# A two-layer hybrid trunk: the FFN's third sums behind the operand's low halves, and the last tile's order of products and stores

## The chip, the cores and the metric

One core of a Trainium2 chip runs the whole program. The metric is the time of one execution on the device, in microseconds (us); lower is better. The core has a matrix engine (TensorE, PE in the profile), a vector engine (VectorE, DVE), an activation engine (ScalarE, ACT), GpSimd (POOL) and SyncE (SP), which issues most transfers. Each engine works through its own queue in order, and they meet through semaphores. SBUF is the memory on the chip, PSUM holds the sums of TensorE.

## What is computed

512 tokens of width 1024 pass through two layers. Cut to what the change touches:

```
x = x + merged @ w_o[i]
h = rmsnorm(x, norm_ffn[i])
x = x + (silu(h @ w_ffn_gate[i]) * (h @ w_ffn_up[i])) @ w_ffn_down[i]
h = rmsnorm(x, norm_ple[i])
x = x + sigmoid(h @ w_ple_gate[i]) * (p[i] @ w_ple_in[i])
...
return rmsnorm(x, norm_final)
```

`merged` comes from an attention, a convolution and a neighbourhood attention under gates; the FFN is 2816 wide. All data are float32.

## The kernel before, in words

**Precision.** An fp32 operand is split into a high half, rounded by ScalarE, and a low half, the rest, made by VectorE (`split`, `operand`). A product is then three matmuls: high by high, high by low, low by high (`mm3`, lines 177 to 179; `product` in `seven`, 983 to 985; `products` in `final`, 1204 to 1206). Activations lie with features on the 128 partitions and 512 tokens along the row, in eight blocks.

**w_o.** `w_o` multiplies the merged operand with eight blocks of output features. The first two blocks go as a pair: 42 matmuls for the first seven operands of both, then the eighth operand, whose halves are the last to be made (the tile mergeb_v, written from gatec_x). Each finished block is added to x, split for the FFN, and squared for the norm. After blocks 2, 4 and 6 `quarters` forms four sums of the operand's blocks (its t1 to t4) and splits them; the last of the four calls stands at the beginning of the FFN.

**FFN.** The 22 blocks of 128 features go in three parts (8, 7, 7). The first block of a part is a plain pair, the gate and the up product. For the others, `seven` gets both products over halves of the tokens and of the inner width from seven half-size products instead of eight, with sums of weights: `s1` and `s2` (up's lower half added to pieces of gate and up by an accumulating transfer of the POOL queue, line 955), and the third sums `s3` = `s1` + a22 (a22 being up's upper half, tile ffn_r) and `s4` = `s3` + the gate's upper half (tile ffn_wr). `s3` and `s4` lie in one place (half of an ffn_qk tile), shared by all blocks, and are split into the tiles ffn_pt or ffn_y.

**What sets the order.** PE's queue is the order of the code. The other engines' queues are set by a planner that knows estimated costs and priorities: weight work is raised in priority (`high_priority`) so that it is placed ahead of the stage that needs it. `behind(i, then)` adds an edge that orders two instructions of one engine without a semaphore. In `seven` the edge puts `s3` behind a22's split, and, where `first` is set (the first such block of parts two and three), behind `self.held`, the last low half of the block before.

**The last tile.** The last layer's final 256 features are computed with tokens on the partitions, in four tiles of 128 tokens (`final`). For a tile: eight times three gate products (`products`), six input products (`inputs`, into PSUM's sc), four transposes of finished features (`chunks`, into tr), and the transposes of 512 more (`low`). `finish` takes the sigmoid on ScalarE, multiplies, adds and sums the squares on VectorE and takes the power -0.5 on GpSimd (line 1228): the column. `store` scales the row by it, on ScalarE for 512 features (line 1235), on VectorE for 256 and 256 (line 1237, which the profile shows under its helper's line 160, and line 1238), and stores each half with one transfer, from the ACT queue (line 1236) and from SP (line 1239).

Of the kernel before, what the change touches and what calls it, by code (L numbers as in the profile page):

```python
# [15 lines left out]
ALU = mybir.AluOpType  # L16
# [9 lines left out]
D = 1024  # L26
# [35 lines left out]
class Net:  # L62
# [848 lines left out]
    def quarters(self, x, h, j):  # L911


        one, two = slice(0, 256), slice(256, 512)
        g = lambda k: self.par(self.i, "ffn", k)
        f = []
        for k in (2 * j, 2 * j + 1):
            v = self.sb("t", [P, 512])
            self.act(v, x[k], AF.Copy, scale=g(k))
            f.append(v)  # L920
        b11, b12, b21, b22 = f[0][:, one], f[0][:, two], f[1][:, one], f[1][:, two]
        u = self.sb("t", [P, 2, 256])
        w = self.sb("t", [P, 2, 256])
        t1, t2, t3, t4 = u[:, 0], u[:, 1], w[:, 0], w[:, 1]
        self.tt(t1, b11, b12, ALU.subtract)
        self.tt(t2, b22, t1, ALU.add)
        self.tt(t3, b22, b12, ALU.subtract)
        self.tt(t4, t2, b21, ALU.subtract)
        if j < 2:
            d = [self.sb("rp" if n < 2 else "e", [P, 2, 256], F32R) for n in range(4)]  # L930
        else:
            d = [q for n in range(2) for q in self.zs[2 * j - 4 + n]]
        for o, t in zip(d, (t1, t2, t3, t4)):
            self.split(o[:, 0], o[:, 1], t)
        ha, hb = self.halves(h[2 * j]), self.halves(h[2 * j + 1])
        cut = lambda p, c: (p[0][:, c], p[1][:, c])
        return dict(b11=cut(ha, one), b21=cut(hb, one), b22=cut(hb, two),
                    **{f"t{n + 1}": (o[:, 0], o[:, 1]) for n, o in enumerate(d)})

    def seven(self, wg, wu, bs, tags, spare, md, first):  # L940


        nc = self.nc
        with self.tc.high_priority(offset=min(self.w_ahead, self.tc.cur_priority - self.p0)):
            lo, up = slice(0, 512), slice(512, 1024)
            g, a22 = self.sb("wr", [P, 1024]), self.sb("r", [P, 512])
            sums = self.sums[self.sevens % 3], self.sums[3]
            self.sevens += 1
            s1, s2, s3, s4 = (s[:, q:q + 512] for s in sums for q in (0, 512))
            nc.sync.dma_start(s1, wg[:, lo])  # L950
            nc.sync.dma_start(s2, wu[:, up])
            nc.sync.dma_start(g, wg)
            nc.sync.dma_start(a22, wu[:, up])
            for q in (s1, s2):
                nc.gpsimd.dma_start(q, wu[:, lo], accum_op=ALU.add)  # L955
            ws = {}

            def halve(hi, lo, src, names):
                i = self.split(hi, lo, src)
                for q, name in enumerate(names):  # L960
                    c = slice(q * 512, q * 512 + 512)
                    ws[name] = (hi[:, c], lo[:, c])
                return i

            wide = lambda: (self.sb("wh", [P, 1024], F32R), self.sb("wl", [P, 1024], F32R))
            halve(*wide(), g, ("a11", "a12"))
            low = halve(self.sb("kh", [P, 512], F32R), self.sb("a", [P, 512], F32R), a22, ("a22",))
            halve(*wide(), sums[0], ("s1", "s2"))
            i = self.tt(s3, s1, a22, ALU.add)
            self.behind(i, low)  # L970
            if first:
                self.behind(i, self.held)
            self.tt(s4, s3, g[:, up], ALU.add)
            halve(*spare, sums[1], ("s3", "s4"))
# [64 lines left out]
    def ffn(self, h, x):  # L1039
        self.phase = "ffn"  # L1040
        i = self.i
# [5 lines left out]
        for part in PARTS:  # L1047
            mids = []
            for f, fb in enumerate(part):
                tags = (("mm", "mm", "mm"), ("sc", "sc", "av"))[fb % 2]  # L1050
                md = md8[f]
                mids.append(md)
                wg, wu = self.a["w_fg"][i, fb], self.a["w_fu"][i, fb]
                if fb:
                    self.seven(wg, wu, bs, tags, spare[fb % 2], md, part[0] and f < 2)
                    continue
                g = self.sb("t", [P, 512])
                pg, pu = (self.ps(t) for t in tags[:2])
                for j in range(len(QUARTERS), 4):
                    self.four.append(self.quarters(x, h, j))  # L1060
                self.pair((pg, pu), (wg, wu), [h[k] for k in ORDER])

                def gate(pg=pg, g=g):
                    self.tt(g, pg, self.rb, ALU.mult)
                    self.act(g, g, AF.Silu, table="silu")

                self.ready(gate)

                def up(pu=pu, g=g, md=md):
                    self.tt(g, g, pu, ALU.mult)  # L1070
                    self.split(md[:, 0, :], md[:, 1, :], g)

                self.ready(up)
# [103 lines left out]
    def final(self, h, x, pairs, hn, most):  # L1177
# [36 lines left out]
        def finish(t):  # L1214
            g = self.sb("t", [P, 256])
            self.act(g, pgs[t], AF.Sigmoid, table="sigmoid", scale=rbs[:, t:t + 1])
            self.tt(g, g, pis[t], ALU.mult)
            v = self.sb("a", [P, 256])
            self.tt(v, g, pair[t][:, 256:], ALU.add)
            q = self.sb("t", [P, 256])  # L1220
            s = self.sb("s", [P, 1])
            nc.vector.tensor_tensor_reduce(
                out=q, in0=v, in1=v, scale=1.0, scalar=0.0, op0=ALU.mult, op1=ALU.add,
                accum_out=s)
            ms = self.sb("sm", [P, 1])
            self.stt(ms, s, 1.0 / D, part[:, t:t + 1], ALU.mult, ALU.add)
            col = self.sb("rc", [P, 1])
            nc.gpsimd.tensor_tensor(col, ms, self.power[:, 0:1], ALU.pow)
            vs.append(v)
            columns.append(col)  # L1230

        def store(t):
            col, two = columns[t], pair[t]
            r, out = rows[t], self.a["out"][t * P:(t + 1) * P]
            self.act(r[:, 0:512], low[t], AF.Copy, scale=col)
            nc.scalar.dma_start(out[:, 0:512], r[:, 0:512])
            self.stt(r[:, 768:], vs[t], col, self.gain, ALU.mult, ALU.mult)
            nc.vector.tensor_scalar(r[:, 512:768], two[:, 0:256], col, None, ALU.mult)
            nc.sync.dma_start(out[:, 512:], r[:, 512:])

        pair, low, pgs, vs, columns = [], [], [], [], []
        places = ("av", "mm", "av", "sc")
        def inputs(t):
            pis.append(self.ps("sc", (P, 256)))
# [6 lines left out]
        for t in range(4):  # L1251
# [10 lines left out]
            if t == 1:  # L1262
# [3 lines left out]
                       start=True, stop=True)  # L1266
                part = self.sb("sm", [P, 4])
                nc.vector.tensor_scalar(part, sums, 1.0 / D, EPS, ALU.mult, ALU.add)
            if t:
                chunks(t)  # L1270
            if t > 1:
                inputs(t)
            products(pg, wg, h, t, range(6, 8))
            pgs.append(pg)
            if t == 1:
                finish(0)
# [130 lines left out]
```

## Time and profile before

| | us |
|---|---|
| time, median of 3 runs (lowest to highest) | 1793.07 (1792.29 to 1793.09) |
| profiled execution, its own time | 1792.81 |
| its span, from first to last instruction | 1791.0 |
| PE busy | 1774.5 |
| DVE busy | 1410.6 |
| ACT busy | 891.6 |
| POOL busy | 99.3 |
| DMA, mean | 142 GB/s |

A row of a time line gives the start (us from the span's start), the duration, the engine, the line of the kernel, the operation, the tile written and the tiles read with shapes, and in brackets the idle time of the engine before it with what ended it. Tiles carry the name of their stage: wo_mm is a PSUM tile of the w_o stage, ffn_qk an SBUF tile of the FFN. Matmuls overlap: one of 512 columns is shown with 0.39 us, and the next starts 0.23 us behind it. "SPq" and "ACTq" are transfers issued by these queues. Line numbers are those of the kernel before.

### The profile page before, as it was taken

What the parts mean: (1) busy time and instruction counts of PE and PEld (TensorE: products, weight loads), DVE (VectorE), ACT (ScalarE), POOL (GpSimd) and SP (SyncE); (2) the same over time, 40 slices, a digit from 0 to 9 for tenths busy, and PEclk for the clock granted to TensorE, in tenths of its full rate; (3) what the DMA queues carried; (4) which work ended last, traced back from release to release, by engine and by line L of the source; (5) the groups of instructions that cost most, each with busy time, mean ns of one, the idle gap of its engine ahead of it and who ended that gap; (6) DMA issues with size and microseconds to landing.
All of it is one profiled execution on the core that took longest, in us unless ns stands there. A gap on an engine that the chain in (4) does not pass through costs nothing.

```text
span 1791.0 us, 27255 instructions
## 1 busy us (share of the span) xinstructions
PE 1774.5 (99%) x10138; PEld 1559.7 (87%) x10138; DVE 1410.6 (79%) x2394; ACT 891.6 (50%) x1551; POOL 99.3 (6%) x142
## 2 busy tenths in 40 slices
PE   9999999999999999999999999999999999999998
PEld 7888888888799899998888888888887998989987
DVE  7877888997788587787776788889887885877776
ACT  5577555325565254454535765552355652534444
POOL 0000000000111011100000000000001110101000
PEclk9999999999999999999999999999999999999999
DMA  5665541334747365544447655422356563746332
GB/s 206 190 182 169 159 124 46 108 98 150 217 130 188 111 166 154 140 123 127 145 125 200 170 161 148 112 71 95 97 182 186 153 173 108 182 133 159 98 103 94
DMA packets 112212, 254.48 MB, mean 142 GB/s; under 512 B 14416, under 2 KB 19024, under 8 KB 112080
## 3 DMA queue, kind: packets, MB, share of 16 engines
q1 hardware_dynamic: 99264, 229.40, 41.9%
q0 software_dynamic: 12096, 22.03, 7.8%
q8 instruction: 80, 1.31, 0.3%
q10 hardware_dynamic: 720, 1.31, 0.2%
q14 instruction: 52, 0.43, 0.1%
HBM read 213.89 MB, written 7.34 MB: 124 GB/s over the span
## 4 chain that ended last, share of the span: by engine, by line
PE 91%; DVE 4%; DMA 2%; ACT 2%; issue 1%; SPq 0%; DVEq 0%; POOLq 0%; ACTq 0%
PE ffn_mm L177 5%; PE ffn_mm L178 5%; PE ffn_mm L179 5%; PE ffn_mm L985 4%; PE ffn_mm L984 4%; PE ffn_mm L983 4%; PE ffn_sc L985 3%; PE ffn_sc L984 3%; PE ffn_sc L983 3%; PE mergea_mm L178 2%; PE mergea_mm L179 2%; PE mergea_mm L177 2%; PE diff_sc L784 2%; PE gatec_mm L177 2%; PE gatec_mm L178 2%; PE gatec_mm L179 2%
## 5 line engine op out<-in xcount | busy, mean ns | idle before, releaser
L160 DVE SCALAR_TENSOR_TENSOR conv_z<-glu_z,pre_par,conv_z 128x512 f32<-128x512 f32 x240 | 179.6, 748 | 3.3
L143 ACT ACTIVATE ffn_wh<-ffn_wr 128x1024 fp32r<-128x1024 f32 (+1 forms) x94 | 94.9, 1015 | 110.0 <-PE ffn_mm L178 75.1
L157 DVE TENSOR_TENSOR ffn_wl<-ffn_wr,ffn_wh 128x1024 fp32r<-128x1024 f32 (+1 forms) x94 | 109.9, 1174 | 5.1 <-ACT ffn_wh L143 4.6
L955 POOL DMA_DIRECT2D ffn_qk<-w_fu x84 | 74.6, 996 | 550.5 <-DMA ffn_qk<-w_fu 218.1
L157 DVE TENSOR_TENSOR ffn_t<-ffn_mm,wo_rb 128x512 f32<-128x512 f32 (+1 forms) x66 | 40.0, 607 | 68.3 <-PE ffn_mm L179 68.3
L143 ACT ACTIVATE mergea_wh<-mergea_wr 128x1024 fp32r<-128x1024 f32 (+1 forms) x32 | 27.1, 846 | 96.8 <-PE mergea_mm L178 79.5
L177 PE MATMUL ffn_mm<-ffn_v,ffn_wh 128*128 128x512 f32 x176 | 68.5, 389 | 0.0
L178 PE MATMUL ffn_mm<-ffn_v,ffn_wh 128*128 128x512 f32 x176 | 68.5, 389 | 0.0
L179 PE MATMUL ffn_mm<-ffn_v,ffn_wl 128*128 128x512 f32 x176 | 68.5, 389 | 0.0
L157 DVE TENSOR_TENSOR ffn_wl<-ffn_qk,ffn_wh 128x1024 fp32r<-128x1024 f32 x42 | 51.4, 1225 | 19.9 <-ACT ffn_wh L143 19.9
L143 ACT ACTIVATE ffn_wh<-ffn_qk 128x1024 fp32r<-128x1024 f32 x42 | 44.5, 1060 | 43.7 <-PE ffn_mm L178 24.5
L157 DVE TENSOR_TENSOR ffn_t<-ffn_t,ffn_t 128x512 f32<-128x512 f32 (+1 forms) x48 | 31.4, 659 | 32.1 <-ACT ffn_t L143 31.5
L143 ACT ACTIVATE diff_a<-diff_sc,diff_s 128x512 f32<-128x512 f32 x32 | 22.0, 687 | 59.0 <-DVE diff_s L875 59.0
L983 PE MATMUL ffn_sc<-wo_h,ffn_wh 128*128 128x256 f32 x176 | 50.0, 284 | 0.0
L985 PE MATMUL ffn_sc<-wo_h,ffn_wl 128*128 128x256 f32 x176 | 49.8, 283 | 0.0
L984 PE MATMUL ffn_sc<-wo_h,ffn_wh 128*128 128x256 f32 x176 | 49.8, 283 | 0.0
L143 ACT ACTIVATE natten_wh<-natten_wr 128x1024 fp32r<-128x1024 f32 x24 | 25.4, 1058 | 41.4 <-issue 15.2
L984 PE MATMUL ffn_mm<-wo_h,ffn_wh 128*128 128x256 f32 x160 | 45.3, 283 | 0.0
L985 PE MATMUL ffn_mm<-wo_h,ffn_wl 128*128 128x256 f32 x160 | 45.3, 283 | 0.0
L983 PE MATMUL ffn_mm<-wo_h,ffn_wh 128*128 128x256 f32 x160 | 45.3, 283 | 0.0
L875 DVE TENSOR_REDUCE diff_s<-diff_sc 128x1 f32<-128x512 f32 x64 | 42.0, 684 | 3.5 <-PE diff_sc L784 3.4
L143 ACT ACTIVATE ffn_kh<-ffn_r 128x512 fp32r<-128x512 f32 x42 | 26.6, 632 | 32.8 <-PE ffn_mm L984 16.2
(825 smaller groups left out, 6577.0 us busy)
## 6 DMA issues: line engine op xcount, KB each, us to landing
ffn_wr<-w_fg SPq DMA_DIRECT2D x44, 512.0 KB, 3.9
ffn_qk<-w_fu POOLq DMA_DIRECT2D x84, 256.0 KB, 5.5
ffn_wr<-w_fd SPq DMA_DIRECT2D x32, 448.0 KB, 3.8
ffn_r<-w_fu SPq DMA_DIRECT2D x42, 256.0 KB, 4.8
ffn_qk<-w_fg SPq DMA_DIRECT2D x42, 256.0 KB, 3.9
ffn_qk<-w_fu SPq DMA_DIRECT2D x42, 256.0 KB, 4.2
natten_wr<-w_in SPq DMA_DIRECT2D x16, 512.0 KB, 4.1
natten_b<-bias SPq DMA_DIRECT2D x32, 256.0 KB, 3.8
```

Of the source, the lines that this page charges most:

```text
L143: i = self.nc.scalar.activation(out, in_, func, **kw)
L157: return self.nc.vector.tensor_tensor(out, a, b, op)
L160: return self.nc.vector.scalar_tensor_tensor(out, a, s, b, op0, op1)
L177: mm(out, wh, ah, start=first, stop=False)
L178: mm(out, wh, al, start=False, stop=False)
L179: mm(out, wl, ah, start=False, stop=last)
L784: self.nc.tensor.matmul(out, st4[:, u, qs], st[:, ks], start=n == 0, stop=n == 1)
L875: nc.vector.tensor_reduce(out=m[:, u:u + 1], in_=sc, op=ALU.max, axis=AX.X, negate=True)
L955: nc.gpsimd.dma_start(q, wu[:, lo], accum_op=ALU.add)
L983: mm(out, wh[:, c], bh, start=first and k == 0, stop=False, skip_group_check=True)
L984: mm(out, wh[:, c], bl, start=False, stop=False, skip_group_check=True)
L985: mm(out, wl[:, c], bh, start=False, stop=k == 3, skip_group_check=True)
```

## The change

```
@@ quarters
         for o, t in zip(d, (t1, t2, t3, t4)):
-            self.split(o[:, 0], o[:, 1], t)
+            self.held = self.split(o[:, 0], o[:, 1], t)
@@ seven
-    def seven(self, wg, wu, bs, tags, spare, md, first):
+    def seven(self, wg, wu, bs, tags, spare, md, first, fb):
...
             i = self.tt(s3, s1, a22, ALU.add)
             self.behind(i, low)
-            if first:
+            if first or fb < 3:
                 self.behind(i, self.held)
@@ ffn
-                    self.seven(wg, wu, bs, tags, spare[fb % 2], md, part[0] and f < 2)
+                    self.seven(wg, wu, bs, tags, spare[fb % 2], md, part[0] and f < 2, fb)
@@ final, finish
-            self.stt(ms, s, 1.0 / D, part[:, t:t + 1], ALU.mult, ALU.add)
+            summed.append(self.stt(ms, s, 1.0 / D, part[:, t:t + 1], ALU.mult, ALU.add))
@@ final, store
-            self.stt(r[:, 768:], vs[t], col, self.gain, ALU.mult, ALU.mult)
+            i = self.stt(r[:, 768:], vs[t], col, self.gain, ALU.mult, ALU.mult)
+            if t == 2:
+                self.behind(i, summed[3])
+            if t == 3:
+                nc.sync.dma_start(out[:, 768:], r[:, 768:])
             nc.vector.tensor_scalar(r[:, 512:768], two[:, 0:256], col, None, ALU.mult)
-            nc.sync.dma_start(out[:, 512:], r[:, 512:])
+            c = slice(512, 768 if t == 3 else D)
+            nc.sync.dma_start(out[:, c], r[:, c])
@@ final, order of a tile's products
-            if t:
+            if t in (1, 2):
                 chunks(t)
-            if t > 1:
+            if t == 2:
                 inputs(t)
             products(pg, wg, h, t, range(6, 8))
+            if t == 3:
+                inputs(t)
+                chunks(t)
```

In the first part of the FFN, the first two blocks that use `seven` now have their third sums ordered behind the last low half that `quarters` has made. In the last tile the remaining six gate products come first, the input products and the transposes behind them; tile 2's scaled features on VectorE (line 1237 of before) come behind the mean of tile 3; and the VectorE half of the last store goes in two transfers.

VectorE's queue around the end of the merge, in layer 0, before (ffn_qk_4946 is `s3` of the FFN's second block, mergeb_v_4549 the low half of the last merged operand, wo_x the sums with w_o's product):

```order
L157 TENSOR_TENSOR mergeb_v_4525<-gatec_x_3070,mergeb_v_4525 128x512
L157 TENSOR_TENSOR gatec_x_3070<-gatec_x_3070,gateb_v_4278 128x512
L157 TENSOR_TENSOR ffn_qk_4946<-ffn_qk_4945,ffn_r_5052 128x512
L157 TENSOR_TENSOR mergeb_v_4549<-gatec_x_3070,mergeb_v_4549 128x512
L157 TENSOR_TENSOR wo_x_4556<-wo_x_4556,wo_mm_4558 128x512
```

The `s3` row is gone from this place in the change, and the two rows around it stand next to each other.

VectorE's queue at the FFN's norm, layer 0, a piece of the difference (wo_z are the last low halves of `quarters`, wo_sm the norm's sum and mean, ffn_wr_5051 the gate weights that `s4` reads, ffn_pt_4936 the low half of `s3` and `s4`, ffn_wl_5068 that of `s1` and `s2`):

```order
 L157 TENSOR_TENSOR wo_z_4554<-ffn_t_4954,wo_z_4554 128x256
 L157 TENSOR_TENSOR wo_z_4555<-ffn_t_4955,wo_z_4555 128x256 x2
+L157 TENSOR_TENSOR ffn_qk_4946<-ffn_qk_4945,ffn_r_5052 128x512
 L215 TENSOR_REDUCE wo_sm_5009<-wo_tr_5004 128x4
+L157 TENSOR_TENSOR ffn_qk_4946<-ffn_qk_4946,ffn_wr_5051 128x512
 L218 TENSOR_SCALAR wo_sm_5011<-wo_sm_5009 128x4
+L157 TENSOR_TENSOR ffn_pt_4936<-ffn_qk_4946,ffn_pt_4935 128x1024
 L157 TENSOR_TENSOR ffn_wl_5068<-ffn_qk_4945,ffn_wh_5067 128x1024
 L157 TENSOR_TENSOR ffn_wl_5185<-ffn_wr_5176,ffn_wh_5184 128x1024
```

`s3`, `s4` and their split come here, `s4` and the split from the middle of the w_o stage. Layer 1 moves in the same way. On SP the next load of ffn_r (for the FFN's fourth block), which needs a slot that `s3` reads, moves behind three loads of x, two of w_o and five of FFN weights.

VectorE's queue at the end of the program, a piece of the difference (ple_y_17675 is tile 2's output row, ple_y_17676 that of tile 3, ple_sm_17896 the mean of tile 3):

```order
-L160 SCALAR_TENSOR_TENSOR ple_y_17675<-ple_a_17837,ple_rc_17844,ple_b_17557 128x256
-L1238 TENSOR_SCALAR ple_y_17675<-ple_tr_17816,ple_rc_17844 128x256
-L157 TENSOR_TENSOR ple_t_17888<-ple_t_17888,ple_sc_17875 128x256
-L157 TENSOR_TENSOR ple_a_17891<-ple_t_17888,ple_tr_17870 128x256
+L1242 TENSOR_SCALAR ple_y_17675<-ple_tr_17816,ple_rc_17844 128x256
+L157 TENSOR_TENSOR ple_t_17888<-ple_t_17888,ple_sc_17876 128x256
+L157 TENSOR_TENSOR ple_a_17891<-ple_t_17888,ple_tr_17883 128x256
 L1222 ISA ple_t_17893,ple_s_17894<-ple_a_17891 128x256
 L1222 ISA ple_s_17894 128x1
 L160 SCALAR_TENSOR_TENSOR ple_sm_17896<-ple_s_17894,ple_sm_17750 128x1
+L160 SCALAR_TENSOR_TENSOR ple_y_17675<-ple_a_17837,ple_rc_17844,ple_b_17557 128x256
 L160 SCALAR_TENSOR_TENSOR ple_y_17676<-ple_a_17891,ple_rc_17898,ple_b_17557 128x256
```

Tile 2's row of line 160 has moved behind the mean of tile 3, which in turn stands one operation earlier. On PE the last six gate products move ahead of six input products and four transposes.

More of the change, by code (lines that the diff above doesn't have):

```diff
@@ L1236, in store @@
             nc.scalar.dma_start(out[:, 0:512], r[:, 0:512])
-            self.stt(r[:, 768:], vs[t], col, self.gain, ALU.mult, ALU.mult)
+            i = self.stt(r[:, 768:], vs[t], col, self.gain, ALU.mult, ALU.mult)
[3 more added lines that the diff above has]
+                nc.sync.dma_start(out[:, 768:], r[:, 768:])
             nc.vector.tensor_scalar(r[:, 512:768], two[:, 0:256], col, None, ALU.mult)
-            nc.sync.dma_start(out[:, 512:], r[:, 512:])
-        pair, low, pgs, vs, columns = [], [], [], [], []
+            c = slice(512, 768 if t == 3 else D)
+            nc.sync.dma_start(out[:, c], r[:, c])
+        pair, low, pgs, vs, columns, summed = [], [], [], [], [], []
         places = ("av", "mm", "av", "sc")
```

## The prediction

> **What bounds the kernel now.** I read the page first, then the waits of TensorE, then the time lines of the two places that the change touches.
>
> ```profile
> span 1791.0 us, 27255 instructions
> ...
> PE 1774.5 (99%) x10138; PEld 1559.7 (87%) x10138; DVE 1410.6 (79%) x2394; ACT 891.6 (50%) x1551; POOL 99.3 (6%) x142
> ...
> PE wo_mm L178 <- DVE mergeb_v L157: 6.0, 2, 3.6
> ```
>
> TensorE (PE) is busy for all but 16.5 us, so an edit pays only where PE waits, or behind its last product. The waits of PE (total, times, longest) have one row of size: 6.0 us in two waits, one per layer, for the low half of the last merged operand. In layer 0 VectorE (DVE) and PE read:
>
> ```profile
> 456.99 0.69 DVE L157 TENSOR_TENSOR gatec_x<-gatec_x,gateb_v 128x512 f32<-128x512 f32 x1
> 465.96 0.69 DVE L157 TENSOR_TENSOR ffn_qk<-ffn_qk,ffn_r 128x512 f32<-128x512 f32 x1 [8.29 <-DMA ffn_qk<-w_fu]
> 466.57 0.69 DVE L157 TENSOR_TENSOR mergeb_v<-gatec_x,mergeb_v 128x512 fp32r<-128x512 f32 x1
> ...
> 457.71 0.63 ACT L143 ACTIVATE mergeb_v<-gatec_x 128x512 fp32r<-128x512 f32 x1 [1.70 <-DVE gatec_x L157]
> ...
> 463.14 0.39 PE L179 MATMUL wo_mm<-mergeb_v,wo_wl 128*128 128x512 f32 x1
> 463.37 0.39 PE L177 MATMUL wo_mm<-mergeb_v,wo_wh 128*128 128x512 f32 x1
> 467.31 0.50 PE L178 MATMUL wo_mm<-mergeb_v,wo_wh 128*128 128x512 f32 x1 [3.56 <-DVE mergeb_v L157]
> ...
> 467.88 0.40 PE L177 MATMUL wo_mm<-mergeb_v,wo_wh 128*128 128x512 f32 x1
> ```
>
> DVE runs its queue in order. The first third sum of the FFN (`s3`, written to ffn_qk) stands ahead of mergeb_v's low half and waits 8.29 us for the accumulating transfer. The low half, whose inputs were there at 458.34 (457.71 + 0.63), is made at 466.57, and PE's L178 waits. Layer 1 repeats it, with a second loss:
>
> ```profile
> 1351.64 0.69 DVE L157 TENSOR_TENSOR ffn_qk<-ffn_qk,ffn_r 128x512 f32<-128x512 f32 x1 [7.18 <-DMA ffn_qk<-w_fu]
> ...
> 1350.15 0.39 PE L177 MATMUL wo_mm<-mergeb_v,wo_wh 128*128 128x512 f32 x1
> 1352.99 0.75 PE L178 MATMUL wo_mm<-mergeb_v,wo_wh 128*128 128x512 f32 x1 [2.46 <-DVE mergeb_v L157]
> 1353.55 0.63 PE L179 MATMUL wo_mm<-mergeb_v,wo_wl 128*128 128x512 f32 x1
> ...
> 1356.52 0.39 PE L177 MATMUL wo_mm<-mergeb_y,wo_wh 128*128 128x512 f32 x1
> ...
> 1353.00:1356.50 3.50, 3.50 (x8) 0.51 1.09 233
> ```
>
> The last row is a window of PE (busy, instructions, granted clock, DMA share, GB/s): after the wait the clock was 0.51 for 3.5 us.
>
> **The third sums.** Price of the stall: PE steps at 0.23 us (463.14 to 463.37). Layer 0: from 463.37 to 467.88 are three steps (one matmul is left out), 4.51 - 0.69 = 3.82 us lost. Layer 1: from 1350.15 to 1356.52 are nine steps (the eight matmuls of the window lie between), 6.37 - 2.07 = 4.30, of which 2.84 - 0.23 = 2.61 is the wait and 1.69 the slow clock. Sum 8.1 us. With `s3` gone from that place the low half ends at about 458.35 + 0.69 = 459.0; PE wants it at 463.60, so 4.6 us are spare, and the whole stall should go.
>
> [...]
>
> Where the sums go, and what they could delay there (`s3`, `s4` and the split into ffn_pt now stand around the FFN's norm):
>
> ```profile
> 508.09 0.69 DVE L215 TENSOR_REDUCE wo_sm<-wo_tr 128x4 f32<-128x512 f32 x1
> 508.88 0.17 DVE L218 TENSOR_SCALAR wo_sm<-wo_sm 128x4 f32<-128x4 f32 x1
> 512.98 1.22 DVE L157 TENSOR_TENSOR ffn_wl<-ffn_qk,ffn_wh 128x1024 fp32r<-128x1024 f32 x1 [3.93 <-ACT ffn_wh L143]
> ...
> 509.13 1.03 POOL L222 TENSOR_TENSOR wo_rc<-wo_sm,pre_power 128x4 f32<-128x4 f32 x1 [38.93 <-DVE wo_sm L218]
> ...
> 512.59 0.60 PE L226 MATMUL wo_tr<-pre_ident,wo_rc 128*128 128x128 f32 x4
> ...
> 492.85 1.22 DVE L157 TENSOR_TENSOR ffn_pt<-ffn_qk,ffn_pt 128x1024 fp32r<-128x1024 f32 x1
> ...
> 520.22 0.28 PE L983 MATMUL ffn_sc<-wo_rp,ffn_pt 128*128 128x256 f32 x1
> ...
> 516.95 0.62 ACT L143 ACTIVATE ffn_kh<-ffn_r 128x512 fp32r<-128x512 f32 x1
> ```
>
> In times of before: one sum ahead of the reduce and one between it and the tensor_scalar, two steps of about 0.6 (465.96 to 466.57), delay the norm by 1.2 us. wo_rc ended at 510.16 and PE wants it at 512.59, 2.43 spare: hidden. ffn_pt's high half on ScalarE (ACT) then runs at about 510.2 to 511.2 and its low half on DVE at 511.2 to 512.4, inside the 3.93 us that DVE waits anyway; PE first reads ffn_pt at 520.22. In addition DVE loses about 1.7 us of work (`s4` and the split at 492.85) ahead of the norm, so it comes to the norm earlier. Cost 0. If that cover were gone, each microsecond would be paid on PE, once per layer.
>
> What waits for `s3` and `s4`: the slot of ffn_r, and the slot of ffn_wr that `s4` reads. The next a22 load (SP's queue) is issued at about 508 instead of 466.68, then the next gate load at about 510; behind them in SP's queue stand the sums' loads of later blocks. The a22 load must have landed when ACT splits it at 516.95, and loads of this kind land within 4.8 us (median) to 6.1:
>
> ```profile
> 466.68 0.33 SPq L953 DMA_DIRECT2D ffn_r<-w_fu  x1
> ...
> DMA to landing us min/median/max: 2.2/4.8/6.1
> ```
>
> At worst 514.4, so 2.5 us are spare. The x loads that stood behind this load in SP's queue go out 8 us earlier.
>
> **The last tile.** PE and the chain behind it:
>
> ```profile
> 1781.52 0.38 PE L1211 MATMUL ple_tr<-pre_ident,ple_h 128*128 128x128 f32 x2
> ...
> 1782.67 0.28 PE L1204 MATMUL ple_mm<-ple_wh,ffn_z 128*128 128x256 f32 x1
> ...
> 1783.59 0.47 ACT L143 ACTIVATE ple_t<-ple_mm,ffn_rc 128x256 f32<-128x256 f32 x1 [3.06 <-PE ple_mm L1206]
> ...
> 1782.84 0.48 DVE L160 SCALAR_TENSOR_TENSOR ple_y<-ple_a,ple_rc,ple_b 128x256 f32<-128x256 f32 x1 [0.74 <-POOL ple_rc L1228]
> 1783.24 0.48 DVE L1238 TENSOR_SCALAR ple_y<-ple_tr,ple_rc 128x256 f32<-128x256 f32 x1
> 1784.09 0.42 DVE L157 TENSOR_TENSOR ple_t<-ple_t,ple_sc 128x256 f32<-128x256 f32 x1 [0.38 <-ACT ple_t L143]
> ...
> 1785.47 0.16 DVE L160 SCALAR_TENSOR_TENSOR ple_sm<-ple_s,ple_sm 128x1 f32<-128x1 f32 x1
> 1786.35 0.48 DVE L160 SCALAR_TENSOR_TENSOR ple_y<-ple_a,ple_rc,ple_b 128x256 f32<-128x256 f32 x1 [0.72 <-POOL ple_rc L1228]
> ...
> 1787.07 0.34 ACTq L1236 DMA_DIRECT2D out<-ple_y  x1
> ```
>
> The gate's last six products move from 1782.67 to 1781.52, so the sigmoid starts at 1782.44, 1.15 earlier. Not all of that arrives. DVE is free for the product with the gate after tile 2's L1238 alone, which moves up to 1782.84 and takes a step of 0.40: 1783.24. Input products and transposes together take PE the 1.15 us that they took before (1781.52 to 1782.67), now from 1782.24 on with the products first; the last transpose is there at about 1783.6, just before the add wants it (1783.69). So the chain moves up by 1784.09 - 1783.24 = 0.85 us.
>
> Against that: tile 2's scaled sum (L160, 0.48 us) now starts right behind the mean of tile 3 and runs while GpSimd (POOL) takes the power. Nearest rows:
>
> ```profile
> 312.66 0.75 DVE L160 SCALAR_TENSOR_TENSOR conv_z<-glu_z,pre_par,conv_z 128x512 f32<-128x512 f32 x1
> ...
> 312.77 1.50 POOL L222 TENSOR_TENSOR diff_rc<-diff_sm,pre_power 128x4 f32<-128x4 f32 x1 [29.29 <-DVE diff_sm L160]
> ...
> 220.34 1.02 POOL L222 TENSOR_TENSOR diff_rc<-diff_sm,pre_power 128x4 f32<-128x4 f32 x1 [58.88 <-DVE diff_sm L160]
> ```
>
> With a DVE operation of two tensors from SBUF beside it, the same power took 0.48 longer, for 0.64 us of overlap. Here the overlap is about 0.3 (the power starts 0.30 behind the mean, the sum 0.12 behind it): between 0 and 0.48, I take 0.2. [...]
>
> The stores. The transfers of the last tile (busy tenths in 40 slices of 0.1 us from 1787.0):
>
> ```profile
> DMA  0000000006999999999999300000000000000000
> ```
>
> They run from about 1787.9 to 1789.3, 1.4 us for two times 256 KB, 2.95 us after the column was ready, and start 0.85 after ACT's issue at 1787.07. In pieces, SP can issue the first 128 KB at 0.51 after the column, packets from 1.36; then 1.4 us of data end at 2.76 if the engines never run dry. That is 0.19 less; a third issue or slower small rows may eat it, so 0 to 0.19, I take 0.1. The tail: 0.85 - 0.2 + 0.1 = 0.75, bounds 0.35 to 1.04.
>
> **Sum.** 8.1 + 0.75 = 8.9 us. The profiled execution took 1792.81 (span 1791.0 and 1.8 around it), 0.26 below the median 1793.07; taken from the median: **1784.2 us**, 0.5% less.
>
> **Rivals.** Clock: the 1.69 us are of one execution. If the timed runs of before fall into no slow clock, the gain is 7.2 and the time 1785.9; if they do in both layers, 1782.5. For it: layer 0's longer wait kept full clock. Against: the three times of before lie within 0.8 us.
>
> The norm: if the two sums make it later than the 2.43 us allow, say by 1 us per layer (the power slowed by 0.48 beside `s4`, and DVE no earlier than before), the time is 1786.2. Against: 1.2 + 0.48 is below 2.43.
>
> Slower than before: the a22 load. It hangs on `s3` now, at the head of SP's queue. If it lands after 516.95, ACT stands, and all weight splits queue behind. It decides the case from 4.5 us late per layer (half of 8.9), a landing 13 us behind `s3`; at 6 us late, 1784.2 + 12 = 1796.2. For it: the load is issued 41 us later than before. Against: the longest landing is 6.1.
>
> No effect: something else holds the low half, PE's wait stays and only the tail comes: 1792.3. Against: on DVE nothing but `s3` stands between gatec_x and it.
>
> **Chances.** Forecast 0.73, clock 0.13, norm 0.07, no effect 0.04, slower 0.03. The clock rival and the tail's bounds reach from 1782.4 to 1786.4; the norm adds little, and with 1786.6 less than 0.2 are left out. About 0.2% (3.6 us) is what a measurement can tell from no change: faster 0.93, same 0.04, slower 0.03.
>
> **What would show it.** Right: no wait of PE on mergeb_v; no half clock in the stage of w_o; the sums' row beside L215; the power of the last tile longer than 0.54; span near 1782. Wrong: a wait of PE at L226 or on ffn_wr's or ffn_r's splits in the first FFN blocks, an idle DVE at `s3`'s new place, or the column of tile 3 no earlier against PE's last product.

## The result and the profile after

| | before | after |
|---|---|---|
| median (lowest to highest), us | 1793.08 (1792.29 to 1794.02) | 1784.24 (1783.78 to 1784.88) |
| profiled execution, us | 1792.81 | 1784.52 |
| its span, us | 1791.0 | 1782.5 |

The ratio is 0.9949, 95% interval 0.9933 to 0.9965: 8.8 us less. Forecast were 8.9 and 1784.2.

The head of the changed kernel's page, and the first rows of its waits of PE (total, times, longest):

```profile
span 1782.5 us, 27275 instructions
...
PE 1772.8 (99%) x10138; PEld 1559.1 (87%) x10138; DVE 1410.6 (79%) x2394; ACT 891.4 (50%) x1551; POOL 99.4 (6%) x142
```

```profile
PE natten_tr L709 <- ACT natten_e L143: 1.2, 2, 0.7
PE pre_av L323 <- DVE pre_zeror L379: 1.1, 1, 1.1
```

The row of 6.0 us for mergeb_v is gone, and no row has taken its place. VectorE's queue at the end of the merge, layer 0, in the time line after:

```profile
457.45 0.69 DVE L157 TENSOR_TENSOR gatec_x<-gatec_x,gateb_v 128x512 f32<-128x512 f32 x1
458.84 0.69 DVE L157 TENSOR_TENSOR mergeb_v<-gatec_x,mergeb_v 128x512 fp32r<-128x512 f32 x1 [0.70 <-ACT mergeb_v L143]
464.71 1.37 DVE L157 TENSOR_TENSOR wo_x<-wo_x,wo_mm 128x512 f32<-128x512 f32 x2 [5.18 <-PE wo_mm L179]
```

The low half now waits 0.70 us for its high half and for nothing else. VectorE then stands idle for 5.18 us, which costs nothing, since PE is busy. Windows of PE after, one in layer 0 and two in layer 1 (length, busy, instructions, granted clock, DMA share, GB/s):

```profile
463.00:466.00 3.00, 3.00 (x15) 1.00 1.10 262
1346.00:1349.00 3.00, 3.00 (x15) 1.00 1.06 252
1349.00:1352.00 3.00, 3.00 (x15) 1.00 1.11 262
```

There is no idle time and no half clock here in either layer. The FFN's norm after, layer 0:

```profile
504.28 0.69 DVE L157 TENSOR_TENSOR ffn_qk<-ffn_qk,ffn_r 128x512 f32<-128x512 f32 x1
504.88 0.69 DVE L215 TENSOR_REDUCE wo_sm<-wo_tr 128x4 f32<-128x512 f32 x1
505.00 0.33 SPq L953 DMA_DIRECT2D ffn_r<-w_fu  x1
505.48 0.69 DVE L157 TENSOR_TENSOR ffn_qk<-ffn_qk,ffn_wr 128x512 f32<-128x512 f32 x1
506.08 0.17 DVE L218 TENSOR_SCALAR wo_sm<-wo_sm 128x4 f32<-128x4 f32 x1
506.34 1.03 POOL L222 TENSOR_TENSOR wo_rc<-wo_sm,pre_power 128x4 f32<-128x4 f32 x1 [35.72 <-DVE wo_sm L218]
...
509.20 0.60 PE L226 MATMUL wo_tr<-pre_ident,wo_rc 128*128 128x128 f32 x4
...
513.56 0.61 ACT L143 ACTIVATE ffn_kh<-ffn_r 128x512 fp32r<-128x512 f32 x1
```

Both sums stand around the reduce, as the queue said. The column wo_rc ends at 507.37 (506.34 + 1.03), 1.83 us before PE wants it, instead of 2.43 before the change. The last tile after:

```profile
1774.53 0.28 PE L1206 MATMUL ple_mm<-ple_wh,ffn_z 128*128 128x256 f32 x1
1774.85 0.47 ACT L143 ACTIVATE ple_t<-ple_mm,ffn_rc 128x256 f32<-128x256 f32 x1 [1.93 <-PE ple_mm L1206]
1775.24 0.48 DVE L1242 TENSOR_SCALAR ple_y<-ple_tr,ple_rc 128x256 f32<-128x256 f32 x1 [0.74 <-POOL ple_rc L1228]
1775.64 0.42 DVE L157 TENSOR_TENSOR ple_t<-ple_t,ple_sc 128x256 f32<-128x256 f32 x1
1776.16 0.42 DVE L157 TENSOR_TENSOR ple_a<-ple_t,ple_tr 128x256 f32<-128x256 f32 x1
...
1777.09 0.16 DVE L160 SCALAR_TENSOR_TENSOR ple_sm<-ple_s,ple_sm 128x1 f32<-128x1 f32 x1
1777.16 0.48 DVE L160 SCALAR_TENSOR_TENSOR ple_y<-ple_a,ple_rc,ple_b 128x256 f32<-128x256 f32 x1
1777.39 0.65 POOL L1228 TENSOR_TENSOR ple_rc<-ple_sm,pre_power 128x1 f32<-128x1 f32 x1 [2.19 <-DVE ple_sm L160]
1778.08 0.48 DVE L160 SCALAR_TENSOR_TENSOR ple_y<-ple_a,ple_rc,ple_b 128x256 f32<-128x256 f32 x1 [0.44 <-POOL ple_rc L1228]
```

The product with the gate follows tile 2's scaling without idle time, and GpSimd's power takes 0.65 us where it takes 0.54 without the scaled sum beside it.

**Where the time went.** The PE queues of both kernels hold the same 10138 matmuls, so starts can be compared one by one, as long as the order is the same. Before layer 0's stall the changed run was 0.46 us late (mostly waits of the neighbourhood attention, which differ from execution to execution: those on natten_e come to 0.8 us in before and 1.2 after); behind it, 3.39 early. Before layer 1's stall it was 3.22 early; behind it, and to the last product, 7.58. So layer 0 gave 3.85 and layer 1 gave 4.36; the other 0.63 of these 8.21 us were lost outside the stalls, 0.46 ahead of the first and 0.17 between the two. The rest lies behind PE's last product, which here and below is the start of its last matmul, a transpose of tile 3. There three steps can be told apart: until the column of tile 3 is ready (the end of the last power), until the last packet of the last store, and until the end of the program.

| us from PE's last product | to the column | column to last data | last data to end | all |
|---|---|---|---|---|
| before | 2.17 | 3.04 | 1.68 | 6.89 |
| after | 1.47 | 2.89 | 1.61 | 5.97 |

7.58 + 0.92 = 8.5 us, which is the difference of the spans.

### The profile page after: what moved, and what is told of

The parts are those of the page before. It is cut to its first block, busy times and chain, and to the rows that moved or that the text cites. A ratio compares the mean times of both kernels' runs of the same rounds, so it can differ in the third digit from the quotient of the medians.

```text
span 1782.5 us, 27275 instructions
## 1 busy us (share of the span) xinstructions
PE 1772.8 (99%) x10138; PEld 1559.1 (87%) x10138; DVE 1410.6 (79%) x2394; ACT 891.4 (50%) x1551; POOL 99.4 (6%) x142
## 4 chain that ended last, share of the span: by engine, by line
PE 93%; DVE 3%; ACT 2%; DMA 1%; issue 1%; POOL 0%; ACTq 0%; SPq 0%; POOLq 0%; DVEq 0%
PE ffn_mm L177 5%; PE ffn_mm L178 5%; PE ffn_mm L179 5%; PE ffn_mm L985 4%; PE ffn_mm L984 4%; PE ffn_mm L983 4%; PE ffn_sc L985 3%; PE ffn_sc L984 3%; PE ffn_sc L983 3%; PE mergea_mm L177 2%; PE mergea_mm L179 2%; PE mergea_mm L178 2%; PE diff_sc L784 2%; PE gatec_mm L177 2%; PE gatec_mm L178 2%; PE gatec_mm L179 2%
## 5 line engine op out<-in xcount | busy, mean ns | idle before, releaser
L985 PE MATMUL ffn_sc<-wo_h,ffn_wl 128*128 128x256 f32 x176 | 49.8, 283 | 0.0
L985 PE MATMUL ffn_mm<-wo_h,ffn_wl 128*128 128x256 f32 x160 | 45.3, 283 | 0.0
```

The lines of the kernel that those rows point to most:

```text
L985: mm(out, wl[:, c], bh, start=False, stop=k == 3, skip_group_check=True)
```

## The experiments

All but two were timed for themselves, beside runs of the kernel before on the same chip. That kernel had medians of 1794.8 to 1795.5 us there, 1.7 to 2.5 above the 1793.1 of the first comparison. The section on what was not expected comes back to that.

### The sums' part alone

The hunks of `quarters`, `seven` and `ffn` as in the change, the last tile as before:

```
-            self.split(o[:, 0], o[:, 1], t)
+            self.held = self.split(o[:, 0], o[:, 1], t)
...
-            if first:
+            if first or fb < 3:
```

> The kernel before with the third sums ordered behind the quarters' low halves, and the last tile left as it was. Stall theory: PE's two waits for mergeb_v (3.82 and 4.30 us with the slow clock behind the second) are the whole gain outside the tail: 8.1 us less than before, about 1785.0, no wait of PE on mergeb_v, full clock in the w_o stage of both layers, and the same distance as before (about 2.2 us) between PE's last product and tile 3's column. Rival, the tail theory (most comes from the last tile): within 1 us of before.

Measured: 1785.03 us (1784.57 to 1785.57) against 1795.31, ratio 0.9945, interval 0.9932 to 0.9957. No wait on mergeb_v, and PE's last product 7.58 us earlier than in the profiled run of before, the same as with the whole change. Behind it 6.88 us, as before. So the stall is all of the gain on PE.

### The last tile's part alone

The hunks of `final` as in the change, `seven` as before:

```
-            if t:
+            if t in (1, 2):
                 chunks(t)
-            if t > 1:
+            if t == 2:
                 inputs(t)
             products(pg, wg, h, t, range(6, 8))
+            if t == 3:
+                inputs(t)
+                chunks(t)
```

(and the edge behind the mean and the stores in pieces.)

> The kernel before with the last tile's new order and stores, and the third sums left where they were. Stall theory: both waits of PE on mergeb_v stay (6.0 us in two), and only the tail's 0.75 to 0.95 us are gained: about 1792.2; a ratio that timing can hardly tell from 1. Tail theory: over 4 us less than before.

Its waits of PE, and three windows of PE in layer 1:

```profile
PE wo_mm L178 <- DVE mergeb_v L157: 5.5, 2, 3.3
```

```profile
1349.50:1352.50 3.00, 0.00 (x0) 1.00 1.13 229
1352.80:1356.20 3.40, 3.40 (x9) 0.50 0.99 196
1356.40:1359.40 3.00, 3.00 (x15) 1.00 0.90 261
```

The stalls are there, 2.15 us in layer 0 and 3.31 in layer 1, the second followed by half clock. Behind PE's last product the program takes 5.98 us, 0.91 less than before: in the trace the tail gives what it gives in the whole change. The times don't show it: 1793.63 (1790.73 to 1798.57) against 1795.31, ratio 0.9995, interval 0.9986 to 1.0004. The two kernels with the stall in them scatter over 6 to 8 us here, and 0.9 us drown in that.

### One instruction: the first sum only changes places with the low half

Instead of past the norm, `s3` goes behind the last low half of the merge alone:

```
@@ merge_b
-            self.split(mg[:, 0, :], mg[:, 1, :], acc[m])
+            self.held = self.split(mg[:, 0, :], mg[:, 1, :], acc[m])
@@ seven
-            if first:
+            if first or fb < 3:
```

(the last tile as before.)

> The kernel before, with the third sum ordered only behind the low half of the last merged operand: it changes places with that one instruction; s4 and the split stay in the w_o stage, and the tail is that of before. VectorE still stands for the transfer, now with nothing that PE needs soon behind it. Stall theory: it is that one instruction that counts, so 8.1 us less than before, about 1785.0, as with the sums behind the quarters; VectorE waits some 6 us for the transfer behind the low half; the sums with w_o's product come 1 to 2 us late and cost PE nothing. Rival, the load theory (it pays that s4 and the split, 1.7 us of VectorE, leave the w_o stage, or VectorE's stop itself costs PE later): a stall of 1 us or more per layer stays, 1787 or more.

VectorE in layer 0:

```profile
458.35 0.69 DVE L157 TENSOR_TENSOR mergeb_v<-gatec_x,mergeb_v 128x512 fp32r<-128x512 f32 x1 [0.70 <-ACT mergeb_v L143]
465.75 0.69 DVE L157 TENSOR_TENSOR ffn_qk<-ffn_qk,ffn_r 128x512 f32<-128x512 f32 x1 [6.71 <-DMA ffn_qk<-w_fu]
466.36 1.28 DVE L157 TENSOR_TENSOR wo_x<-wo_x,wo_mm 128x512 f32<-128x512 f32 x2
```

VectorE still waits 6.71 us for the accumulating transfer, and it costs nothing now, because PE wants nothing of VectorE in that time. 1784.54 us (1784.39 to 1785.25), ratio 0.9944, interval 0.993 to 0.9957. Two neighbouring instructions exchanged give the same as the change's long way past the norm. In the traces this exchange, once per layer, is the only difference between the queues of this kernel and of before, the transfers included. That in the change the load of ffn_r goes out 38 us later, or the x loads 8 us earlier, therefore has no part in the gain.

### One layer at a time

The sums' part in layer 0 only, and in layer 1 only (the last tile as before):

```
-            if first:
+            if first or (fb < 3 and self.i == 0):
```

> Only layer 0's third sums stand behind the low halves; layer 1 and the last tile are as before. Theory (each layer pays for its own s3, and what one layer gains reaches the end): PE's waits have one row for mergeb_v, in layer 1, of 2.4 to 3.4 us; in layer 0 no idle and full clock; PE's last product 3.8 us earlier than before, a little less (3.2) if the waits of the neighbourhood attention, which follows, grow back; 3.2 to 3.8 us off the median where the clock treats both alike. The times still scatter by several us between runs, because one stall that may meet the half clock (1.7 us, or 3.4 for two such windows) is left. Rival (the layers are coupled: an earlier layer 0 makes layer 1's weights wait): layer 1's wait grows beyond 3.5 us and under 2 us arrive.

```
-            if first:
+            if first or (fb < 3 and self.i == 1):
```

> Only layer 1's third sums stand behind the low halves; layer 0 and the last tile are as before. Theory: one row for mergeb_v is left, in layer 0, of 2.1 to 3.7 us; layer 1 without idle and at full clock; PE's last product 4.3 us earlier than before (2.6 of wait and 1.7 of half clock as in the profiled run of before). The part of the clock is not sure of every run: 2.6 to 6 us off the median, and a scatter of some us while one stall is left; together with the kernel that moves layer 0's sums alone it must come to what both layers gave (about 8 in the profiled runs, 9 to 10 in these timed ones). Rival (the first layer's stall sets all, the second is only its echo): layer 1's move gives under 1 us.

Layer 0's sums alone: 1790.62 us (1788.35 to 1791.8), 4.2 below the before of that job (1794.78), ratio 0.9973, interval 0.9962 to 0.9983. Layer 1's alone: 1789.18 (1788.45 to 1790.43), 5.6 below, ratio 0.9967, interval 0.9955 to 0.998. Together 9.8. Forecast were 3.2 to 3.8 and 2.6 to 6; layer 0's 4.2 lies above its range, which was given for a clock that treats both kernels alike. The first kernel, in the waits of PE and the half-clock window of layer 1:

```profile
PE wo_mm L178 <- DVE mergeb_v L157: 3.4, 1, 3.4
```

```profile
1351.00:1354.40 3.40, 3.40 (x9) 0.53 1.01 190
```

And PE of the second, in layer 0:

```profile
463.25 0.39 PE L177 MATMUL wo_mm<-mergeb_v,wo_wh 128*128 128x512 f32 x1
466.78 0.80 PE L178 MATMUL wo_mm<-mergeb_v,wo_wh 128*128 128x512 f32 x1 [3.14 <-DVE mergeb_v L157]
```

```profile
466.30:473.00 6.70, 6.22 (x15) 0.51 1.01 235
473.20:476.20 3.00, 3.00 (x15) 1.00 1.11 275
```

In the first kernel layer 0 gave 3.86 us on PE (from 0.49 late to 3.37 early), and layer 1 kept its stall, 0.9 us longer than in before (3.38 instead of 2.46). In the second, layer 1 gave 4.37, and layer 0's stall of 3.14 us was followed by 6.8 us of half clock, which before's stall of 3.56 in the same place was not. So each layer pays for its own `s3`, layer 1 is no echo of layer 0, and the price of one stall is the wait and nothing, one or two stretches of 3.4 us at half clock.

### The sums still later

The changed kernel, with `s3` of the first block behind the low half of `s1` and `s2` too, past the norm:

```
-            halve(*wide(), sums[0], ("s1", "s2"))
+            low2 = halve(*wide(), sums[0], ("s1", "s2"))
...
+            if fb == 1:
+                self.behind(i, low2)
```

> The changed kernel with the first third sum later still, behind the low half of s1 and s2, after the norm. The norm is then free of the sums, and the a22 load of the FFN's fourth block, which needs the slot that s3 reads, is issued some 6 us later (about 511 instead of 505), at a place where ScalarE has its split early in its queue. Queue theory (the slower rival of the prediction): the load lands at about 516, ScalarE stands some 4 us at that split, the copies of the second block's products and the gate's SiLU wait behind it, PE waits 2 to 3 us per layer: about 1789 to 1791. Rival (the loads have room): 1784.2 as the changed kernel, and the norm 1.2 us earlier in VectorE's queue.

Its waits of PE, then windows of PE, then ACT's time line, all in layer 0 but for the first row (line numbers are 2 higher than in the changed kernel, the wait is named at product L985):

```profile
PE ffn_av L985 <- ACT ffn_t L143: 6.3, 2, 3.4
```

```profile
510.00:517.20 7.20, 4.74 (x40) 1.00 0.78 213
517.20:524.05 6.85, 5.96 (x28) 0.50 0.83 214
524.05:527.00 2.95, 2.95 (x26) 1.00 0.95 185
```

```profile
512.37 1.06 ACT L143 ACTIVATE ffn_pt<-ffn_qk 128x1024 fp32r<-128x1024 f32 x1 [1.47 <-DVE ffn_qk L157]
513.73 0.63 ACT L143 ACTIVATE ffn_kh<-ffn_r 128x512 fp32r<-128x512 f32 x1 [0.29 <-DMA ffn_r<-w_fu]
514.38 1.28 ACT L143 ACT_TABLE_LOAD   x1
515.67 0.63 ACT L143 ACTIVATE ffn_t<-ffn_t 128x512 f32<-128x512 f32 x1
516.21 1.04 ACT L143 ACTIVATE ffn_wh<-ffn_qk 128x1024 fp32r<-128x1024 f32 x1
517.15 0.61 ACT L143 ACTIVATE ffn_v<-ffn_t 128x512 fp32r<-128x512 f32 x1
517.67 0.36 ACT L143 ACTIVATE ffn_t<-ffn_av 128x256 f32<-128x256 f32 x1
```

The last of these rows in the changed kernel:

```profile
514.09 0.36 ACT L143 ACTIVATE ffn_t<-ffn_av 128x256 f32<-128x256 f32 x1
```

1794.63 us (1793.32 to 1795.63), ratio to before 0.9997, interval 0.9988 to 1.0006: the whole gain is gone. The load of ffn_r, issued at 510.63, cost 0.29 us. What PE waited for, 3.35 and 2.95 us, is ACT's copy of ffn_av, which frees a PSUM tile. The late sums put three splits ahead of it that stand elsewhere in the changed kernel: the one into ffn_pt (512.37, for which ACT waited 1.47 us), one of weights (516.21) and one of activations (517.15). The copy ended at 518.03 (517.67 + 0.36) instead of 514.45 in the changed kernel, although this run was 0.8 us ahead of that one before. Each wait met half clock again, 6.8 us in layer 0 and 3.4 in layer 1: on PE the two layers lost 6.2 and 4.7 us against the changed kernel. Waits of 2 to 3 us were foreseen, but by way of the load; the clock's part was not, and the time came out above the 1789 to 1791 that were expected.

### The scaled sum ahead again, and the other half behind

The changed kernel without the edge behind the mean of tile 3:

```
-            if t == 2:
-                self.behind(i, summed[3])
```

> The changed kernel, but tile 2's scaled sum stands ahead of tile 3's product again (no edge behind the mean). Theory of the prediction: the power of tile 3 takes 0.54 instead of 0.65, and the column of tile 3 comes 0.3 later against the end of the gate's last product: 0.40 of DVE's step lost, 0.11 of POOL's contention won. Rival (DVE has a gap there anyway, since it waits 0.74 for tile 2's column): 0.40 lost only in part, and the column no later than 0.1.

And the changed kernel with the edge on the other scaling of tile 2, which reads PSUM and the column, while the sum with two operands from SBUF goes ahead:

```
-            i = self.stt(r[:, 768:], vs[t], col, self.gain, ALU.mult, ALU.mult)
-            if t == 2:
-                self.behind(i, summed[3])
+            self.stt(r[:, 768:], vs[t], col, self.gain, ALU.mult, ALU.mult)
...
-            nc.vector.tensor_scalar(r[:, 512:768], two[:, 0:256], col, None, ALU.mult)
+            i = nc.vector.tensor_scalar(r[:, 512:768], two[:, 0:256], col, None, ALU.mult)
+            if t == 2:
+                self.behind(i, summed[3])
```

> The changed kernel, but behind the mean of tile 3 VectorE does the scaling that reads PSUM and the column, and the sum with two operands from SBUF goes ahead of tile 3's product. Theory (what slows GpSimd's power is a VectorE operation with two operands from SBUF beside it): the power takes 0.54 with VectorE as busy beside it as in the changed kernel, and the column comes 0.1 earlier against the gate's last product: 3.41 instead of 3.52. Rival (any VectorE work beside it does): 0.65 and 3.52. The time differs by 0.1 us either way, less than these runs can tell.

The power of tile 3, first with the sum ahead, then VectorE and the power with the PSUM scaling behind:

```profile
1777.96 0.54 POOL L1228 TENSOR_TENSOR ple_rc<-ple_sm,pre_power 128x1 f32<-128x1 f32 x1 [2.57 <-DVE ple_sm L160]
```

```profile
1777.14 0.48 DVE L1240 TENSOR_SCALAR ple_y<-ple_tr,ple_rc 128x256 f32<-128x256 f32 x1
...
1777.36 0.54 POOL L1228 TENSOR_TENSOR ple_rc<-ple_sm,pre_power 128x1 f32<-128x1 f32 x1 [2.19 <-DVE ple_sm L160]
```

Three cases of the same power: nothing beside it, 0.54 us; an operation of 0.48 that reads PSUM beside it, 0.54; one of 0.48 with two operands from SBUF, 0.65. So it is not that VectorE is busy. What decides is what its operation reads, or the operation itself (TENSOR_SCALAR the one, SCALAR_TENSOR_TENSOR the other), which these runs do not separate. The price is 0.11 us here. Two operands from SBUF alone are not enough, as another power of before shows:

```profile
417.12 0.43 DVE L157 TENSOR_TENSOR pin_wl<-pin_wr,pin_wh 128x256 fp32r<-128x256 f32 x1 [0.59 <-ACT pin_wh L143]
416.70 1.01 POOL L222 TENSOR_TENSOR conv_rc<-conv_sm,pre_power 128x4 f32<-128x4 f32 x1 [102.42 <-PE pin_sc L178]
```

It kept its 1.01 us beside an operation that reads two SBUF tiles but began 0.42 us behind it. In the two cases that took longer VectorE's operation was already under way, and the power grew by the overlap less some 0.15 us (0.48 for 0.64 in the prediction's rows, 0.11 for 0.25 here).

The kernel without the edge ran once, in 1785.00 us. Without the edge the column comes 0.28 us later than in the changed kernel (3.79 instead of 3.52 from the gate's last product); with the edge on the other scaling 0.11 earlier (3.41).

### One store, and the place of the last one

The changed kernel with one transfer for the VectorE half of the last tile:

```
-            if t == 3:
-                nc.sync.dma_start(out[:, 768:], r[:, 768:])
...
-            c = slice(512, 768 if t == 3 else D)
+            c = slice(512, D)
```

> The changed kernel, but the SP half of the last tile goes in one transfer again. Theory: the last data come 3.0 us after the column instead of 2.6, and the end of the program follows 1.7 behind the last data instead of 1.9: the span against PE's last product is 0.2 to 0.4 longer. Rival (the last data hang on ACT's half, whose issue is not moved): no difference in the last data.

The 2.6 and 1.9 that stand for the changed kernel in this expectation were misread; by the packets they are 2.89 and 1.61, as in the table above. This kernel ran once, in 1784.82 us. With one store the last data came 3.05 us behind the column, 0.16 later, as the theory has it. But the program ended 1.26 behind the last data, not 1.7. Behind PE's last product it took 5.78 us, 0.2 less than with the pieces. So the same kernel ran again, beside the changed one.

> The kernel with one store for the SP half of the last tile, once more, beside the changed kernel. In its first profile the last data came 3.05 us behind the column instead of 2.89, yet the program ended 1.26 behind the last data instead of 1.61, so that the end was 0.2 us earlier, not later. Theory (the data decide; the 1.26 belongs to one execution): 3.05 again and an end 1.6 to 1.7 behind the data, 0.15 to 0.2 later than in the changed kernel. Rival (fewer transfers at the end let the program end earlier): 1.26 again, and a median 0.2 below that of the changed kernel, if the runs can tell so little.

> The changed kernel itself on the same chip as the two beside it. Expected: 1784.2 to 1785.0 us, all runs within 1.2 us of each other, the power of tile 3 at 0.65, the last data 2.89 behind the column and the end 1.6 behind the data.

Once more 3.04 and 1.25 with one store; the changed kernel repeated its 0.65 for the power, 2.89 and 1.62. Medians: 1783.75 us (1783.44 to 1784.35) with one store, 1784.35 (1783.91 to 1784.69) for the changed kernel. These ranges overlap; the trace is the better witness. It has at the end eight semaphore events of SP, which wait for the eight semaphores that the transfers take in turn. When each was passed, and when the program ended, in us from the last packet:

```
before              0.36  0.43  0.49  0.55  0.61  0.67  0.73  0.79   end 1.68
after               0.11  0.36  0.43  0.49  0.55  0.61  0.67  0.73   end 1.61
one store (again)  -0.26 -0.20 -0.14 -0.07 -0.01  0.05  0.11  0.36   end 1.25
```

In all three a wait is passed 0.36 us after the last packet: the last store's own. It is the first of the eight in before, the second after the change, the eighth with one store. Each wait behind it costs 0.06, and 0.89 follow the eighth. The place depends on how many transfers were counted before and in what order. The last kernel puts pieces and the eighth place together, with the PSUM scaling behind the mean:

```
-            nc.scalar.dma_start(out[:, 0:512], r[:, 0:512])
+            if t > 1:
+                nc.scalar.dma_start(out[:, 0:512], r[:, 0:512])
...
-            c = slice(512, 768 if t == 3 else D)
+            c = slice(512 if t > 1 else 0, 768 if t == 3 else D)
```

> The kernel with the PSUM-reading scaling behind the mean (power at 0.54), and the rows of tiles 0 and 1 stored whole by SP, so that two transfers fewer are counted before the last one. Behind the last data SP waits for eight semaphores of transfers one after another, in a fixed order, at 0.06 us each; the transfers take them in turn. In the changed kernel the last store has the second of the eight, here it would have the eighth. Theory (the six waits behind the last store's are what the end costs): the end follows 1.25 behind the last data as in the kernel with one store, the data still 2.9 behind the column, and PE's last product to the end takes 5.5 instead of 5.97 us (0.11 by the power, 0.37 by the place). Rival (one store less of 128 KB at the end is what made that kernel end early): 1.6 behind the data, 5.9. A median of 1783.6 to 1784.2, some 0.4 below the changed kernel.

It ended 1.25 us behind the last data, which came 2.93 behind the column.

| us from PE's last product | to the column | column to last data | last data to end | all |
|---|---|---|---|---|
| after | 1.47 | 2.89 | 1.61 | 5.97 |
| sum ahead | 1.75 | 2.88 | 1.68 | 6.31 |
| PSUM scaling behind | 1.37 | 2.91 | 1.62 | 5.90 |
| one store (again) | 1.47 | 3.04 | 1.25 | 5.76 |
| pieces, last place | 1.36 | 2.93 | 1.25 | 5.54 |

The theory holds: the place is worth 0.37 us, the pieces 0.1 to 0.15. The rival, that one store less lets the program end early, falls, since this kernel stores both pieces. With the sum ahead the last store has the first of the eight places again, which is 0.07 of the 0.34 us that this kernel needs more than the changed one. The last kernel's median is 1784.14 (1783.74 to 1785.64), ratio to before 0.9938, interval 0.9925 to 0.9952. Its 0.44 us against the changed kernel are seen in the trace, not in the times. The PSUM scaling behind the mean alone had 1784.41 (1784.08 to 1784.51).

## Why the prediction was right

**The stall.** Price 8.1 us, measured on PE 3.85 + 4.36 = 8.2. That it was `s3` alone, is shown by the exchange of two instructions. The low half was forecast at about 459.0 in times of before; it started at 458.84 and ended at 459.53 in a run that was 0.5 late there. The 0.46 us by which the changed run was late before layer 0's stall are the scatter of single executions: in the nine traces without a stall the last product came 6.91 to 8.42 us earlier than in before, while each gained the same 3.85 and 4.37 at the two stalls, to 0.01.

**The norm.** Costed at 0 and hidden: PE has no wait at L226. The column came 0.6 us later against PE, not 1.2, because VectorE reached the norm earlier, as the prediction said without a number. The split into ffn_pt lay in idle time of ACT and VectorE.

**The a22 load.** Issued at 505.00, landed 2.4 us later, needed at 513.56: 6.2 us spare, more than the 2.5 of the worst case. The rival that made the kernel slower was right that too late a sum costs PE through ACT's queue, and the experiment with still later sums shows it. It was wrong in the carrier: the load cost 0.29 us there, the order of ACT's queue 3 us per layer.

**The last tile.** Forecast 0.75, measured 0.92, from parts that were off both ways: the mean 0.05 less, the longer power 0.09 less, the stores 0.12 more. The chain was to move by 0.85: the product moved by 0.87 against PE's last product, the mean by 0.80, since the add (1776.16) waited some 0.06 for the transposes that it reads. What the power takes longer beside the sum was put at 0.2 and was 0.11. The stores in pieces were taken at 0.1; the data came 0.15 earlier (from 3.04 by the packets, where the prediction read 2.95 off the slices) and the end followed 0.07 closer. The transfers of after, in 40 slices of 0.1 us from 1778.5:

```profile
DMA  8999999974999999998999920000000000000000
```

The data end at about 1780.9. Up to the last no slice falls below 4 tenths, so the engines don't run dry between the three transfers, which was the condition for the gain. What the step did not see is that the end of the program hangs on the last store's place among eight waits. It was the first in before and would be the eighth in the change with one store; the pieces made it the second. So one store alone would have been 0.2 us better, not 0.1 worse.

**The clock.** The forecast of 8.9 us took before's one half-clock stretch for every run, the rival let it vary. In the first comparison the forecast held, and as far as the clock goes that was luck: the one trace of before could not tell how many such stretches its timed executions would meet. In the later ones before was slower, the changed kernel was not (1784.35 against 1784.24), and the gain of the same kernel was 10.4 us (1794.76 - 1784.35), near the 10.6 that the rival gave for slow clock in both layers. So the sum's term for the clock, 1.69 us, is right for one set of runs and too small for others.

## What to carry to other kernels

An instruction that waits for a transfer holds up what stands behind it in its engine's queue: `s3` waited 8.29 us in layer 0 of before, and PE 3.56 us for the low half behind it. Look for the one that stands ahead of what TensorE wants next, and exchange the two before anything larger is moved. How far back it may go was set here by the next engine's queue (behind the low half of `s1` and `s2` it cost 6.2 and 4.7 us on PE), so read what its result triggers there. A stall of TensorE can cost more than it lasts, and unevenly: those of 2.15 to 3.56 us had no half clock behind them, or 3.4 or 6.8 us of it. The kernels without one are not only faster, the times of each lie within 2 us.

## What was not expected of the hardware

**Stalls and scatter.** Waits of PE and the half clock behind them in us, from the profiled executions:

| kernel, layer | wait | idle in each step of 3.413 us | half clock behind |
|---|---|---|---|
| before, 0 | 3.56 | 1.85, 1.71 | none |
| before, 1 | 2.46 | 2.46 | 3.4 |
| tail alone, 0 | 2.15 | 1.83, 0.33 | none |
| tail alone, 1 | 3.31 | 0.20, 3.11 | 3.4 |
| layer 0's sums, 1 | 3.38 | 0.40, 2.98 | 3.4 |
| layer 1's sums, 0 | 3.14 | 2.34, 0.80 | 6.8 |
| later sums, 0 | 3.35 | 2.49, 0.86 | 6.8 |
| later sums, 1 | 2.95 | 0.70, 2.26 | 3.4 |

The longest wait, 3.56 us, was followed by no half clock, nor was the shortest, 2.15; waits of 2.46 to 3.38 us were, by 3.4 or 6.8 us of it. The clock's own records in the traces tell when it changed: in before at 4.80, 1353.07, 1356.48 and 1786.56 us, which are 0, 395, 396 and 522 steps of 3.413 us from the first; in after at 6.15 and 1781.08 us, 520 steps apart. The third column cuts each wait at these steps, counted on in its own trace. In the eight waits a step with 2.26 us of idle or more was followed by one at half clock, and none of those with 1.85 or less brought it on. Before's longest wait was cut into 1.85 and 1.71. Where a wait reached 0.80 or 0.86 us into the step at half clock, the next one stayed at half clock too; where it took nothing of that step, full clock came back. Outside the waits, in the traces of before and after, the least idle that was followed by half clock is 2.14 us, where PE's work ends in before. That the idle of a step decides is an estimate of the author from these figures: no run moved a wait against the steps on purpose. The idle times go by the modelled ends of the matmuls.

The 51 later executions of before show the price in their times: at a mean granted clock of 0.996 their median is 1795.95 us (22 runs), at 0.997 1794.6 (14), at 0.998 1793.8 (14). The kernels without a stall ran at 0.999 to 1.000, all of one kernel within 2 us.

**The end of the program.** 1.25 to 1.68 us from the last packet to the last instruction, by the last store's place among eight waits of 0.06 us.

**GpSimd's power beside VectorE.** 0.11 us for an overlap of 0.25 with an operation of two operands from SBUF that was under way, none with one that reads PSUM, and none where two operands from SBUF came 0.42 us behind the power's start.
